# Hybrid conv / RWKV / MoE block on one core: weights laid out in load order, last norm's gain spread by TensorE, other pieces and rings at both ends

## The chip, the cores and the metric

The kernel runs on one core of one Trainium2 chip. The metric is the device time of one execution in microseconds (us), the median of several runs; work on the host before the launch is not in it. Names of engines are those of the profile: PE (matrix multiply), PEld (its weight loads), DVE, ACT, POOL, and SP, which here only issues DMA.

## The reference

One block over 256 tokens of width 2048, all in float32: a mixing half and a mixture of experts with 32 experts of inner width 512.

```
u = rms_norm(x, norm_mix);  proj = u @ w_in                  # w_in 2048 x 5408
y_conv = conformer_conv(proj[:1024], proj[1024:2048], ...)   # 31 taps
y_rwkv = rwkv7_time_mix(proj[2048:], ...)    # the last 288 columns of w_in are low-rank inputs
h = x + concat(y_conv, y_rwkv) @ w_out                       # w_out 2048 x 2048
v = rms_norm(h, norm_ffn)
h = h + moe(v)    # per token 2 of 32 experts:  (silu(v @ w_gate[e]) * (v @ w_up[e])) @ w_down[e]
out = rms_norm(h, norm_final)
```

Every expert has some token here, and the kernel loads all 32: w_gate and w_up (2048 x 512) and w_down (512 x 2048) are 4 MB each, so 403 MB in all.

## The kernel before

**Start.** `norm_in` loads x in four pieces of 512 KB and the 288 low-rank columns of w_in in four pieces, in the order of `STARTS`, squares and sums x, and multiplies the low-rank columns with x already (names `la`, `xn`), so that the statistics and these products lie side by side. The scale of each token is spread over the partitions by a matmul (`rstd`), and only then are the operands `yh` and `yl` of the big projections made.

**Mixing half.** `proj` computes 256 output columns at a time: chunks of 8 row blocks of a weight (128 x 2048 numbers, 1 MB) are loaded, split on ACT and DVE into a high and a low part (`hi`, `lo`), and multiplied three times. Its weights are w_in (20 column blocks, by two chunks each), then w_out (8 column blocks, in `w_out_pass`, the last two row blocks apart in `load_rest`).

**Experts.** They are taken in 16 pairs (`pair`). Both experts of a pair share PE: columns 0 to 63 are slots of one, 64 to 127 of the other. A pair has 24 chunks of 1 MB, in this order: four groups of gate, gate, up, up (one for each expert of the pair), then four quarters of w_down with two chunks each. PE multiplies group by group (tiles `g`, `u`), transposes the hidden layer (`hid`, `hT`), multiplies with w_down (`y`), and adds the rows back to their tokens with 0/1 matrices (`cb`, `acc`). The next pair's tokens are gathered (`gt`, `xe`) between these.

**Rings.** Chunks go to buffers in a fixed cycle of 21, written by `ORDER` from five groups: A, B, C, D and E. A is the ring that the first half streams its weights through (two of its buffers hold x until w_out is done), and `NA` and `NB` say how many A and B have. In the last pair A is taken out, for the last norm uses it (`final_tiles`), and the cycle goes on over what is left, by the chunk's number modulo the length:

```
def ORDER(A, B, C, D, E):
    return C[0:3] + B + A[0:2] + C[3:] + D + A[2:4] + E + A[4:]
r = rings[self.nchunk % len(rings)]                            # expert_chunk
rings = [r for r in rings if r[0] is not self.ring]            # last pair
```

All weights are issued by SP, in program order as the scheduler wrote it. A DMA there waits for the DMA that last used its completion counter (there are eight, taken in turn: the names DMAHW0 to DMAHW7 in the rows of the order below), for PE where the buffer's last reader is a matmul, and holds back everything behind it.

**End.** `expert_down` of the last pair works in the pieces of `LAST`, with `behind=0`: after each piece PE waits for ACT and DVE (`yh`, `yl`), then does its `cb`. `final_part` squares the sums on ACT and multiplies by the gain (`nfb`) on DVE; `final_norm` reduces, scales and stores. PE runs the experts in the order of the program.

Of the kernel before, what the change touches and what calls it, by code (L numbers as in the profile page):

```python
# [31 lines left out]
TAPS = -2500  # L32
LOW = -1500
GATHER = -24
STARTS = (0, 4, 1, 2, 3, 5, 6, 7)
PSTART = ("l0", "l1", "l2", "l3", "s0", "s1", "s2", "s3", "l4", "l5", "b", *(f"l{k}" for k in range(6, 16)))
TOKENS = ((0, 4), (4, 4), (8, 4), (12, 2), (14, 2))
WSLOT = {4: "ylb", 5: "yla", 6: 0, 7: 1}
RING = 1024
NA, NB, ND, NEX = 5, 7, 3, 1  # L40
NXE = 3
CHAIN = 400
QUARTERS = [(512 * i, 512) for i in range(4)]
LAST = QUARTERS[:2] + [(1024, 384), (1408, 384), (1792, 256)]
FINAL = [(i, slice(a, b)) for i in range(2) for a, b in ((0, 512), (512, 1024), (1024, 2048))]


def ORDER(A, B, C, D, E):
# [6 lines left out]
      "conv_b", "ln_g", "ln_b"]  # L55
PCI = {n: i for i, n in enumerate(PC)}
INPUTS = ["xT", "w_in", "w_out", "pc", "dw", "mul", "nmix", "nffn_c", "wa_up", "g_up1", "g_up2",
          "rw", "rb", "nffn_p", "nfin", "w_gate", "w_up", "w_down"]


def bcast_rows(ap, n):
    return bass.AP(tensor=ap.tensor, offset=ap.offset, ap=[[0, 128], [1, n]])
# [13 lines left out]
class Block:  # L76
# [169 lines left out]
        nc.vector.tensor_sub(lo, view, hi.bitcast(F32))  # L246
        return hi, lo

    def proj(self, src, k0, nk, c0, width, xh, xl, x0, cols, slot=None):
        accs = [self.bank(self.pacc, [128, 256], "acc") for _ in cols]  # L250
        rows = src.rearrange("(k p) n -> p k n", p=128)
        for b in range(0, nk, 8):
            nb = min(8, nk - b)
            with self.tc.high_priority(offset=2000):
                c = self.chunk(rows[:, k0 + b:k0 + b + nb, c0:c0 + width], slot)
            for g in range(0, nb, 4):
                ng = min(4, nb - g)
# [12 lines left out]
    def norm_in(self):  # L270
        nc = self.nc
        V, A = nc.vector, nc.scalar
        warm = self.tmp.tile([128, 1], F32, tag="t", name="warm")
        A.activation(warm, self.c_rms, AF.Sqrt)
        xr = self.xT.rearrange("(k p) t -> p k t", p=128)
        wr = self.w_in.rearrange("(k p) n -> p k n", p=128)
        x = lambda k, n: self.xT_s[k // 8][:, k % 8:k % 8 + n]
        wl = []
        for step in STARTS:
            if step < 4:  # L280
                nc.sync.dma_start(x(4 * step, 4), xr[:, 4 * step:4 * step + 4])
            else:
                k = 4 * (step - 4)
                c = self.chunk(wr[:, k:k + 4, O_L:O_L + 288])
                wl += [c[:, j] for j in range(4)]
        xn = [self.rwkv_parts(i, F32, "y") for i in range(2)]
        ss = self.bank(self.pmm, [128, 2], "mm")
        la = [self.bank(self.pacc, [128, 288], "acc") for _ in range(2)]
        sqs = []
        for g in range(4):  # L290
            for k in range(4 * g, 4 * g + 4):
                V.tensor_scalar(xn[k // 8][k % 8], self.xt(k), self.nmix_s[:, k:k + 1], None, op0=OP.mult)
            sq = self.spl.tile([128, 4, 256], F32, tag="hi" if g % 2 else "lo", name="nsq")
            A.activation(sq, x(4 * g, 4), AF.Square)
            V.tensor_add(sq[:, 0:2], sq[:, 0:2], sq[:, 2:4])
            V.tensor_add(sq[:, 0], sq[:, 0], sq[:, 1])
            sqs.append(sq)
        rs = self.lo.tile([128, 2], F32, name="rs")
        dg = self.tmp.tile([128, 2, 128], F32, tag="t", name="dg")
        rstd = self.bank(self.pmm, [128, 256], "mm")  # L300
        last = None

        def ordered(*a, **k):
            nonlocal last
            m = nc.tensor.matmul(*a, **k)
            if last is not None:
                self.after(m, last, sync=False)
            last = m

        for step in PSTART:  # L310
            n = int(step[1:] or 0)
            for i in range(2):
                ts = slice(128 * i, 128 * i + 128)
                if step[0] == "l":
                    ordered(la[i], xn[n // 8][n % 8][:, ts], wl[n], start=n == 0, stop=n == 15)
                elif step[0] == "s":
                    ordered(ss[:, i:i + 1], sqs[n][:, 0, ts], self.ones[:, 0:1],
                            start=n + i == 0, stop=n + i == 4)
                else:
                    if i == 0:  # L320
                        A.activation(rs, ss, AF.Sqrt, bias=self.c_rms, scale=1.0 / D)
                        self.gate_in = V.reciprocal(rs, rs)
                    V.tensor_scalar(dg[:, i], self.ident, rs[:, i:i + 1], None, op0=OP.mult)
                    ordered(rstd[:, ts], self.ones, dg[:, i], start=True, stop=True)
        yh, yl = (Parts([self.ypool.tile([128, 8, 256], F32R, tag=n + h, name=n + h) for h in "ab"], 8)
                  for n in ("yh", "yl"))
        for g in range(8):
            s = slice(2 * g, 2 * g + 2)
            y = xn[g // 4][2 * (g % 4):2 * (g % 4) + 2]
            V.tensor_mul(y, y, rstd[:, None, :].to_broadcast([128, 2, 256]))  # L330
            A.activation(yh[s], y, AF.Copy)
            self.gate_y = V.tensor_sub(yl[s], y, yh[s].bitcast(F32))
        self.yh, self.yl = yh, yl
        self.la, self.rs = la, rs
# [3 lines left out]
                      for h, n in (("a", 6), ("b", 2))], 6)  # L338

    def w_in_cols(self, c0):  # L340
        return self.proj(self.w_in, 0, 16, c0, 256, self.yh, self.yl, 0, (0, 128))

    def shift(self, ps, mu, omu, out):
        nc = self.nc
# [411 lines left out]

    def w_out_pass(self, k0, nk, xh, xl, x0, slots={}):
        for b in range(8):
            ps = self.proj(self.w_out, k0, nk, 256 * b, 256, xh, xl, x0, (0, 128), slots.get(b))
            for i in range(2):  # L760
                h = self.xt(2 * b + i)
                self.nc.vector.tensor_add(h, h, ps[i])

    def load_rest(self):
        self.wrest = []
        for k in (14, 15):
            c = self.ring.tile([128, 2048], F32, tag="w", name="w")
            self.nc.sync.dma_start(c, self.w_out[128 * k:128 * k + 128, :])
            self.wrest.append(c)

    def rest_block(self, b):
# [287 lines left out]
    def wsrc(self, which, e, q):  # L1059
# [1 line left out]
            w = (self.w_gate, self.w_up)[which][e]  # L1061
            return w.rearrange("(p a) f -> p a f", a=16)[:, 4 * q:4 * q + 4, :]
        c0, n = q
        return self.w_down[e].rearrange("(p a) n -> p a n", a=4)[:, :, c0:c0 + n]

    def expert_chunk(self, rings, which, e, q):
        r = rings[self.nchunk % len(rings)]
# [8 lines left out]

    def final_tiles(self):
        nfb, *self.fin = (self.ring.tile([128, D], F32, tag="w", name=n) for n in ("nfb", "fin0", "fin1"))
        self.nc.gpsimd.dma_start(nfb, bcast_rows(self.nfin, D))
        self.nfb = nfb  # L1080
        self.fs1 = self.per.tile([128, 2], F32, name="fs1")
        self.fss = self.per.tile([128, 2, len(LAST)], F32, name="fss")

    def final_part(self, c0, w):
        k = [c for c, _ in LAST].index(c0)
# [47 lines left out]
    def run(self):  # L1133
# [4 lines left out]
        with ExitStack() as top:  # L1138
# [6 lines left out]
            with P("yp", 1, "right") as self.ypool:  # L1145
# [25 lines left out]
                with ExitStack() as ex:  # L1171
# [19 lines left out]
                    with tc.manual_schedule(engines={mybir.EngineType.PE}):  # L1191
                        xe = [self.gather(wk, pg, S, 0, 2)]
                        late = ()
                        for pr in range(NE // 2):
                            load = lambda w, j, q: self.expert_chunk(rings, w, 2 * pr + j, q)
                            last = pr + 1 == NE // 2
                            if last:
                                rings = [r for r in rings if r[0] is not self.ring]
                                self.final_tiles()
                            xe, S, late = self.pair(wk, pg, py, pgu, load, (2 * pr, 2 * pr + 1), xe, S,  # L1200
                                                    None if last else (2 * pr + 2, 2 * pr + 3),
                                                    None if pr else weights, late,
                                                    **(dict(pieces=LAST, after=self.final_part, behind=0)
                                                       if last else {}))
                    self.final_norm()
            self.overflow()

# [1 line left out]
def pack(inputs):  # L1209
    g = {k: np.asarray(v) for k, v in inputs.items()}  # L1210
    f = {}
    f["xT"] = np.ascontiguousarray(g["x"][0].T)
    f["w_in"] = g["w_in"][0]
    f["w_out"] = g["w_out"][0]
    mu = g["shift_mu"][0]
    ch = {"mu_r": mu[0:DC], "mu_k": mu[DC:2 * DC], "mu_v": mu[2 * DC:3 * DC], "w0": g["w0"][0],
          "a0": g["a0"][0], "k_k": g["k_k"][0], "k_a": g["k_a"][0], "r_k": g["r_k"][0].reshape(-1),
# [18 lines left out]
    f["nfin"] = g["norm_final"][None]  # L1236
    f["w_gate"] = g["expert_w_gate"][0]
    f["w_up"] = g["expert_w_up"][0]
    f["w_down"] = g["expert_w_down"][0]
    return {n: f[n] for n in INPUTS}  # L1240


# [11 lines left out]
```

## Time and profile before

| what | value |
|---|---|
| time, median of 3 runs | 1495.16 us (1492.93 to 1495.94) |
| the profiled execution's own time | 1495.7 us |
| its span, first to last instruction | 1493.6 us |
| busy share of the span | PE 94%, PEld 58%, DVE 44%, ACT 27%, POOL 2% |
| chain that ended last | PE 56%, DMA 30%, DVE 10%, ACT 2% |
| HBM read | 468.97 MB, 315 GB/s over the span |
| granted clock of TensorE, mean | 0.99 |

The shares of busy time run over two unlike parts: until about 530 us the mixing half, in which the DMA engines are half idle, and from there on the experts, in which they are busy throughout. A PE that is busy is not a PE at its peak, since matmuls overlap. What limits a stretch is read from the chain and from windows over that stretch.

### The profile page before, as it was taken

Reading aid. Unit: us, or ns where it says so; the run is one execution under the profiler, and the core shown is the slowest. Engines: PE = TensorE matmul, PEld = TensorE weight load, DVE = VectorE, ACT = ScalarE, POOL = GpSimd, SP = SyncE. Lnnn points to the kernel's source line nnn. Section 1 sums busy time; section 2 is a strip of 40 time slices with the busy share of each in tenths; the row PEclk is TensorE's granted clock in tenths of the full one; section 3 lists DMA queues with packets and bytes.
Section 4 is the critical chain, followed back from the end, with each engine's and each line's share of the span. In section 5 each row is a group of like instructions: output and inputs, shape, how many; then the busy total and the mean of one; then the engine's idle time right before and its main releaser. Section 6 shows DMA issues by size and latency. Waiting matters only on the chain.

```text
span 1493.6 us, 21307 instructions
## 1 busy us (share of the span) xinstructions
PE 1402.4 (94%) x8730; PEld 859.6 (58%) x8730; DVE 656.4 (44%) x1350; ACT 409.9 (27%) x758; POOL 30.3 (2%) x66
## 2 busy tenths in 40 slices
PE   7999999999999979999999999999898998989895
PEld 5989988888889944434434434434344344433432
DVE  7797977969867533223223223222131231221314
ACT  5657666676685411001001001001000010000102
POOL 4000000000000000000000000000000000000000
PEclk9999999999999999999999999999999999999998
DMA  7542442432549779999999999999999999999993
GB/s 235 184 149 85 136 130 88 151 101 88 177 128 346 284 292 377 414 412 426 412 418 417 412 422 415 414 421 412 417 421 413 424 412 415 416 409 425 410 412 138
DMA packets 168518, 472.52 MB, mean 316 GB/s; under 512 B 8000, under 2 KB 70512, under 8 KB 135264
## 3 DMA queue, kind: packets, MB, share of 16 engines
q1 hardware_dynamic: 167072, 467.96, 80.4%
q0 software_dynamic: 1200, 3.13, 0.7%
q8 instruction: 71, 1.16, 0.3%
q14 instruction: 31, 0.25, 0.1%
q10 hardware_dynamic: 144, 0.01, 0.0%
HBM read 468.97 MB, written 2.10 MB: 315 GB/s over the span
## 4 chain that ended last, share of the span: by engine, by line
PE 56%; DMA 30%; DVE 10%; ACT 2%; issue 1%; SPq 0%; ACTq 0%; DVEq 0%
DMA w<-in_w_up_dram 21%; PE acc L217 14%; PE u L217 9%; PE y L217 9%; PE g L217 8%; DMA w<-in_w_down_dram 7%; PE mm L217 7%; PE gt L217 5%; PE cb L217 3%; DVE lo L246 3%; DVE mix L642 2%; DVE MB L479 1%; DMA w<-in_w_in_dram 1%; PE cn L217 1%; ACT hi L245 1%
## 5 line engine op out<-in xcount | busy, mean ns | idle before, releaser
L217 PE MATMUL u<-w,xe 128*64 128x512 f32 x1024 | 252.1, 600 | 22.4 <-DMA w<-in_w_up_dram 22.4
L217 PE MATMUL g<-w,xe 128*64 128x512 f32 x1024 | 248.0, 597 | 13.6 <-DMA w<-in_w_gate_dram 11.2
L217 PE MATMUL y<-w,hT 128*64 128x512 f32 (+2 forms) x1040 | 232.5, 594 | 0.7 <-ACT hT L1022 0.7
L1039 DVE TENSOR_TENSOR acc<-acc,cb 128x512 f32<-128x512 f32 (+2 forms) x130 | 86.0, 674 | 218.8 <-PE cb L217 218.8
L217 PEld LDWEIGHTS u<-w,xe 128*64 128x64 f32 x1024 | 81.7, 138 | 173.2 <-issue 129.2
L1014 DVE TENSOR_TENSOR hid<-sg,u 128x256 f32<-128x256 f32 x32 | 19.6, 614 | 346.6 <-PE u L217 346.6
L217 PEld LDWEIGHTS g<-w,xe 128*64 128x64 f32 x1024 | 73.9, 136 | 152.6 <-issue 121.8
L246 DVE TENSOR_TENSOR lo<-w,hi 128x1024 fp32r<-128x1024 f32 x108 | 127.6, 1181 | 46.5 <-ACT hi L245 33.8
L217 PEld LDWEIGHTS y<-w,hT 128*64 128x64 f32 x1040 | 70.6, 137 | 133.7 <-issue 118.3
L1010 ACT ACTIVATE sg<-g 128x512 f32<-128x512 f32 x16 | 9.6, 597 | 482.5 <-PE g L217 482.5
L217 PE MATMUL gt<-S,vt 128*128 128x128 f32 x1024 | 125.9, 279 | 6.8 <-DVE xe L961 5.2
L217 PEld LDWEIGHTS gt<-S,vt 128*128 128x128 f32 x1024 | 120.8, 194 | 14.3 <-DVE xe L961 8.7
L245 ACT ACTIVATE hi<-w 128x1024 fp32r<-128x1024 f32 x108 | 110.8, 1026 | 54.3 <-PE acc L217 45.5
L1052 ACT ACTIVATE yh<-y,gate 128x512 fp32r<-128x512 f32 (+2 forms) x65 | 44.3, 681 | 251.6 <-PE y L217 251.6
L642 DVE SCALAR_TENSOR_TENSOR mix<-UP,dw_s,mix 128x256 f32<-128x256 f32 x240 | 104.0, 477 | 2.7 <-ACT mix L640 2.4
L217 PE MATMUL acc<-yha,hi 128*128 128x256 f32 x320 | 92.1, 288 | 2.5 <-ACT hi L245 1.8
L217 PE MATMUL acc<-yla,hi 128*128 128x256 f32 x320 | 92.5, 289 | 0.0
L217 PE MATMUL acc<-yha,lo 128*128 128x256 f32 x320 | 92.0, 288 | 0.0
L217 PE MATMUL acc<-yhb,lo 128*128 128x256 f32 x320 | 91.9, 287 | 0.0
L217 PE MATMUL acc<-ylb,hi 128*128 128x256 f32 x320 | 91.2, 285 | 0.0
L217 PE MATMUL acc<-yhb,hi 128*128 128x256 f32 x320 | 90.3, 282 | 0.0
L961 DVE TENSOR_TENSOR xe<-gt,nffnp_s 128x512 f32<-128x512 f32 (+1 forms) x65 | 44.4, 683 | 80.9 <-PE gt L217 80.9
(352 smaller groups left out, 1894.2 us busy)
## 6 DMA issues: line engine op xcount, KB each, us to landing
w<-in_w_gate_dram SPq DMA_DIRECT2D x128, 1024.0 KB, 19.1
w<-in_w_up_dram SPq DMA_DIRECT2D x128, 1024.0 KB, 19.5
w<-in_w_down_dram SPq DMA_DIRECT2D x124, 1024.0 KB, 14.2
w<-in_w_in_dram SPq DMA_DIRECT2D x40, 1024.0 KB, 5.2
w<-in_w_out_dram SPq DMA_DIRECT2D x8, 1024.0 KB, 5.8
w<-in_w_out_dram SPq DMA_DIRECT2D x8, 768.0 KB, 4.7
w<-in_w_down_dram SPq DMA_DIRECT2D x4, 768.0 KB, 12.6
w<-in_w_in_dram SPq DMA_DIRECT2D x4, 576.0 KB, 7.4
```

The source lines that it names most:

```text
L217: self.nc.tensor.matmul(*a, **k)
L245: nc.scalar.activation(hi, view, AF.Copy)
L246: nc.vector.tensor_sub(lo, view, hi.bitcast(F32))
L479: V.copy_predicated(MB[:, 2 * h + c], self.mkP.rearrange("p a b -> p (a b)"), P12[h])
L642: V.scalar_tensor_tensor(c, u, d, c, op0=OP.mult, op1=OP.add)
L961: self.nc.vector.tensor_mul(xe[:, a:a + n], ps, self.nffnp_s[:, k0:k0 + n, None].to_broadcast([128, n, 128]))
L1010: A.activation(sg, gp, AF.Silu)
L1014: V.tensor_mul(hid, *(t.rearrange("s (p f) -> s f p", f=4)[:, f:f + 2] for t in (sg, up)))
L1039: V.tensor_add(a, a, cb)
L1052: A.activation(yh, yp, AF.Copy, scale=gate)
```

## The change

- The host stores x, w_in, w_out and w_down in the order in which the kernel loads them. Every load of them is then one unbroken run in HBM, with one long row for each partition (4 to 8 KB), where before a chunk had rows of 1 KB (w_in, w_out, x) or 2 KB (w_down). The numbers that land in SBUF are the same, except for the low-rank columns.
- The low-rank columns come in three loads of 6, 5 and 5 row blocks (before, four of 4), at other places among the pieces of x.
- Ring A has 6 buffers and ring B has 6 (before, 5 and 7). The cycle still has 21; without A the last pair's has 15 (before, 16).
- The gain of the last norm is loaded as one row, and four matmuls with a row of ones spread it over the partitions (`final_gain`, behind the first group of the last pair), with four ACT copies. Before, one DMA read the row 128 times.
- The last w_down goes in pieces of 512, 512, 512, 256 and 256 columns (before 512, 512, 384, 384, 256), and PE does a piece's `cb` after the next piece's `y`.

```
-STARTS = (0, 4, 1, 2, 3, 5, 6, 7)
+STARTS = (0, 4, 1, 2, 5, 3, 6)
+LORA = ((0, 6), (6, 5), (11, 5))
-NA, NB, ND, NEX = 5, 7, 3, 1
+NA, NB, ND, NEX = 6, 6, 3, 1
-LAST = QUARTERS[:2] + [(1024, 384), (1408, 384), (1792, 256)]
+LAST = QUARTERS[:3] + [(1536, 256), (1792, 256)]
...
-                c = self.chunk(rows[:, k0 + b:k0 + b + nb, c0:c0 + width], slot)
+                c = self.chunk(rows[:, k0 + b:k0 + b + nb], slot)
...
             if step < 4:
-                nc.sync.dma_start(x(4 * step, 4), xr[:, 4 * step:4 * step + 4])
+                nc.sync.dma_start(x(4 * step, 4), self.xT[step])
             else:
-                k = 4 * (step - 4)
-                c = self.chunk(wr[:, k:k + 4, O_L:O_L + 288])
-                wl += [c[:, j] for j in range(4)]
+                k, n = LORA[step - 4]
+                c = self.chunk(self.w_lo[:, k:k + n])
+                wl += [c[:, j] for j in range(n)]
...
-        return self.w_down[e].rearrange("(p a) n -> p a n", a=4)[:, :, c0:c0 + n]
+        return self.w_down[e, c0 // 512][:, :, c0 % 512:c0 % 512 + n]
...
-        self.nc.gpsimd.dma_start(nfb, bcast_rows(self.nfin, D))
+        self.nfr = self.fin[0][0:1, :]
+        self.nc.gpsimd.dma_start(self.nfr, self.nfin)
+        self.one_row = self.fin[1][0:1, 0:128]
+        self.nc.vector.memset(self.one_row, 1.0)
...
+    def final_gain(self, pg):
+        for c0, w in QUARTERS:
+            ps = self.bank(pg, [128, w], "gt")
+            self.mm(ps, self.one_row, self.nfr[:, c0:c0 + w], start=True, stop=True)
+            self.nc.scalar.activation(self.nfb[:, c0:c0 + w], ps, AF.Copy)
...
                                 self.final_tiles()
+                                late = [*late, lambda: self.final_gain(pg)]
...
-                                                    **(dict(pieces=LAST, after=self.final_part, behind=0)
-                                                       if last else {}))
+                                                    **(dict(pieces=LAST, after=self.final_part) if last else {}))
+                        for f in late:
+                            f()
...
+    f["w_in"] = np.ascontiguousarray(wi[:, 0:O_L].reshape(16, 128, 20, 256).transpose(2, 1, 0, 3))
+    f["w_lo"] = np.ascontiguousarray(wi[:, O_L:].reshape(16, 128, 288).transpose(1, 0, 2))
+    f["w_out"] = np.ascontiguousarray(wo[0:1792].reshape(14, 128, 8, 256).transpose(2, 1, 0, 3))
+    f["w_down"] = np.ascontiguousarray(
+        g["expert_w_down"][0].reshape(NE, 128, 4, 4, 512).transpose(0, 3, 1, 2, 4))
```

Three places show how the order of instructions moves. The first is SP at the start of the program. `xT_s` is x, `w` a buffer of ring A, and the last row in each is the 40 chunks of w_in. Before:

```order
L281 DMA xT_s<-in_xT_dram 128x4x256
L237 DMA w<-in_w_in_dram 128x4x288
L281 DMA xT_s<-in_xT_dram 128x4x256 x3
L237 DMA w<-in_w_in_dram 128x4x288 x3
L237 DMA w<-in_w_in_dram 128x8x256 x40
```

Now:

```order
L280 DMA xT_s<-in_xT_dram 128x1024
L238 DMA w<-in_w_lo_dram 128x1728
L280 DMA xT_s<-in_xT_dram 128x1024 x2
L238 DMA w<-in_w_lo_dram 128x1440
L280 DMA xT_s<-in_xT_dram 128x1024
L238 DMA w<-in_w_lo_dram 128x1440
L238 DMA w<-in_w_in_dram 128x2048 x40
```

The last piece of x now stands behind the second low-rank load, and one buffer is left over for the first chunk of w_in.

The second is SP where the last pair's loads begin, with what each DMA waits for in brackets (PE: a buffer's last reader). The rows of w_down are the last of the pair before. Before:

```order
L1074 DMA w<-in_w_down_dram 128x4x512 [waits DMAHW0_49,PE_49]
L1074 DMA w<-in_w_down_dram 128x4x512 [waits DMAHW1_49,PE_49]
L1074 DMA w<-in_w_down_dram 128x4x512 [waits DMAHW2_49,PE_49]
L1074 DMA w<-in_w_gate_dram 128x2048 [waits DMAHW3_49,PE_49]
L1074 DMA w<-in_w_gate_dram 128x2048 [waits DMAHW4_49,PE_49]
L1074 DMA w<-in_w_up_dram 128x2048 [waits DMAHW5_49,PE_49]
L1074 DMA w<-in_w_up_dram 128x2048 [waits DMAHW6_49,PE_49]
```

Now:

```order
L1073 DMA w<-in_w_down_dram 128x2048 [waits DMAHW7_49,PE_49]
L1073 DMA w<-in_w_down_dram 128x2048 [waits DMAHW0_49,PE_49]
L1073 DMA w<-in_w_down_dram 128x2048 [waits DMAHW1_49,PE_49]
L1073 DMA w<-in_w_gate_dram 128x2048 [waits DMAHW7_49,DMAHW2_49,PE_49]
L1073 DMA w<-in_w_up_dram 128x2048 [waits DMAHW3_49]
L1073 DMA w<-in_w_gate_dram 128x2048 [waits DMAHW4_49,DMAHW0_49,PE_49]
L1073 DMA w<-in_w_up_dram 128x2048 [waits DMAHW5_49,DMAHW1_49,PE_49]
L1073 DMA w<-in_w_gate_dram 128x2048 [waits DMAHW6_49]
```

The last pair's first, third and fourth load now wait for counters 7, 0 and 1 as well, which are those of the three w_down loads just ahead; and one up chunk stands ahead of the second gate chunk.

The third is PE after the last pair's transposes of `hid`. Before, the end of the program was:

```order
L217 MATMUL y<-w,hT 64x512 x8
L217 MATMUL cb<-yh,ST 128x512
L217 MATMUL cb<-yl,ST 128x512
L217 MATMUL cb<-yh,ST 128x512
L217 MATMUL cb<-yl,ST 128x512
L217 MATMUL y<-w,hT 64x512 x8
```

Now:

```order
L218 MATMUL y<-w,hT 64x512 x16
L218 MATMUL cb<-yh,ST 128x512
L218 MATMUL cb<-yl,ST 128x512
L218 MATMUL cb<-yh,ST 128x512
L218 MATMUL cb<-yl,ST 128x512
L218 MATMUL y<-w,hT 64x512 x8
```

Two pieces of `y` now stand ahead of the first `cb`, and so on to the end, where two groups of `cb` follow each other.

## Rows read from the trace of the kernel before

**Rows 1.** The page: what the DMA engines moved, span in 40 slices.

```profile
GB/s 235 184 149 85 136 130 88 151 101 88 177 128 346 284 292 377 414 412 426 412 418 417 412 422 415 414 421 412 417 421 413 424 412 415 416 409 425 410 412 138
```

**Rows 2.** Windows over the experts; at the right PEclk, DMA share, GB/s.

```profile
530.00:550.00 20.00, 18.07 (x92) 9.49 (x94) 5.87 (x28) 1.59 (x3) 0.00 (x0) 0.88 0.56 207
590.00:900.00 310.00, 308.27 (x1558) 133.74 (x1556) 77.87 (x153) 21.70 (x33) 0.00 (x0) 1.00 1.02 416
```

**Rows 3.** The chain in order of time, experts: start us, us, what.

```profile
634.25 7.02 PE y L217 x32
...
854.41 7.02 PE y L217 x32
...
917.94 19.58 DMA w<-in_w_up_dram
...
957.27 3.65 PE u L217 x14
...
1017.70 3.65 PE u L217 x14
```

**Rows 4.** Windows: w_down moving (963 to 975), gate and up (the others).

```profile
924.00:951.00 27.00, 27.00 (x131) 11.67 (x128) 4.81 (x10) 0.69 (x1) 0.00 (x0) 1.00 1.01 426
963.00:975.00 12.00, 11.65 (x71) 6.45 (x70) 3.71 (x8) 1.49 (x3) 0.00 (x0) 1.00 1.05 394
981.00:1011.00 30.00, 28.73 (x138) 11.20 (x134) 5.90 (x12) 0.69 (x1) 0.00 (x0) 1.00 1.01 425
```

**Rows 5.** The start: the chain in order of time, and one window.

```profile
1.31 5.73 DMA w<-in_w_in_dram
20.07 8.43 DMA w<-in_w_in_dram
32.01 0.55 PE mm L362 x3
5.40:12.00 6.60, 4.83 (x10) 3.50 (x11) 5.80 (x17) 4.05 (x5) 1.48 (x6) 1.00 1.09 351
```

**Rows 6.** The start: the timeline of DVE and ACT.

```profile
18.14 1.88 DVE L330 TENSOR_TENSOR y0a<-y0a,mm 128x512 f32<-128x512 f32 x3 [0.17 <-PE mm L305]
31.48 0.87 ACT L360 ACTIVATE mix<-acc,rs 128x288 f32<-128x288 f32 x2
```

**Rows 7.** The gain's tile `nfb`, and the chain while it loads.

```profile
L1079 POOL DMA_DIRECT2D nfb<-in_nfin_dram x1: 533/533/533, 1376.5 to 1376.5; - x1
...
1363.41 22.16 DMA w<-in_w_up_dram
```

**Rows 8.** PE's timeline over the ends of two pairs; idle before it in brackets.

```profile
1322.14 3.65 PE L217 MATMUL u<-w,xe 128*64 128x512 f32 x14 [1.34 <-DMA w<-in_w_up_dram]
1340.64 3.65 PE L217 MATMUL y<-w,hT 128*64 128x512 f32 x16
1345.35 3.65 PE L217 MATMUL y<-w,hT 128*64 128x512 f32 x16
1385.62 6.55 PE L217 MATMUL u<-w,xe 128*64 128x512 f32 x14 [3.74 <-DMA w<-in_w_up_dram]
```

**Rows 9.** SP's timeline, last pair; DMA issues from 514.2 to 515.2, us to landing.

```profile
1410.72 5.04 SPq L1074 DMA_DIRECT2D w<-in_w_gate_dram  x2
...
w<-in_w_up_dram SPq DMA_DIRECT2D x1, 1024.0 KB, 5.0
```

**Rows 10.** The end: PE's timeline, and two rows of the chain.

```profile
1452.70 5.35 PE L217 MATMUL y<-w,hT 128*64 128x512 f32 x16 [0.74 <-ACT hT L1022]
1460.53 3.65 PE L217 MATMUL y<-w,hT 128*64 128x512 f32 x16
1476.49 1.95 PE L217 MATMUL y<-w,hT 128*64 128x256 f32 x16
861.43 1.12 PE cb L217 x4
1481.83 0.08 DVE fs L1095
```

More of the change, by code (lines that the diff above doesn't have):

```diff
@@ L57 @@
 INPUTS = ["xT", "w_in", "w_out", "pc", "dw", "mul", "nmix", "nffn_c", "wa_up", "g_up1", "g_up2",
-          "rw", "rb", "nffn_p", "nfin", "w_gate", "w_up", "w_down"]
+          "rw", "rb", "nffn_p", "nfin", "w_lo", "w_outr", "w_gate", "w_up", "w_down"]
 def bcast_rows(ap, n):
@@ L247, in split, with proj @@
         return hi, lo
-    def proj(self, src, k0, nk, c0, width, xh, xl, x0, cols, slot=None):
+    def proj(self, rows, k0, nk, xh, xl, x0, slot=None):
+        cols = (0, 128)
         accs = [self.bank(self.pacc, [128, 256], "acc") for _ in cols]
-        rows = src.rearrange("(k p) n -> p k n", p=128)
         for b in range(0, nk, 8):
@@ L274, in norm_in @@
         A.activation(warm, self.c_rms, AF.Sqrt)
-        xr = self.xT.rearrange("(k p) t -> p k t", p=128)
-        wr = self.w_in.rearrange("(k p) n -> p k n", p=128)
         x = lambda k, n: self.xT_s[k // 8][:, k % 8:k % 8 + n]
@@ L340, in w_in_cols @@
     def w_in_cols(self, c0):
-        return self.proj(self.w_in, 0, 16, c0, 256, self.yh, self.yl, 0, (0, 128))
+        return self.proj(self.w_in[c0 // 256], 0, 16, self.yh, self.yl, 0)
     def shift(self, ps, mu, omu, out):
@@ L758, in w_out_pass @@
         for b in range(8):
-            ps = self.proj(self.w_out, k0, nk, 256 * b, 256, xh, xl, x0, (0, 128), slots.get(b))
+            ps = self.proj(self.w_out[b], k0, nk, xh, xl, x0, slots.get(b))
             for i in range(2):
@@ L765, in load_rest @@
         self.wrest = []
-        for k in (14, 15):
+        for k in range(2):
             c = self.ring.tile([128, 2048], F32, tag="w", name="w")
-            self.nc.sync.dma_start(c, self.w_out[128 * k:128 * k + 128, :])
+            self.nc.sync.dma_start(c, self.w_outr[128 * k:128 * k + 128])
             self.wrest.append(c)
@@ L1211, in pack @@
     f = {}
-    f["xT"] = np.ascontiguousarray(g["x"][0].T)
-    f["w_in"] = g["w_in"][0]
-    f["w_out"] = g["w_out"][0]
+    f["xT"] = np.ascontiguousarray(g["x"][0].T.reshape(4, 4, 128, T).transpose(0, 2, 1, 3))
+    wi, wo = g["w_in"][0], g["w_out"][0]
+    f["w_in"] = np.ascontiguousarray(wi[:, 0:O_L].reshape(16, 128, 20, 256).transpose(2, 1, 0, 3))
+    f["w_lo"] = np.ascontiguousarray(wi[:, O_L:].reshape(16, 128, 288).transpose(1, 0, 2))
+    f["w_out"] = np.ascontiguousarray(wo[0:1792].reshape(14, 128, 8, 256).transpose(2, 1, 0, 3))
+    f["w_outr"] = np.ascontiguousarray(wo[1792:])
     mu = g["shift_mu"][0]
@@ L1238, in pack @@
     f["w_up"] = g["expert_w_up"][0]
-    f["w_down"] = g["expert_w_down"][0]
+    f["w_down"] = np.ascontiguousarray(
+        g["expert_w_down"][0].reshape(NE, 128, 4, 4, 512).transpose(0, 3, 1, 2, 4))
     return {n: f[n] for n in INPUTS}
```

## The prediction, made before the result

> **What bounds the kernel now.** I read the page's slices first. In [rows 1] the slices of 37 us show a DMA rate of 85 to 346 GB/s in the first fourteen, the mixing half, and of 409 to 426 from the sixteenth to the one before the last. The first windows [rows 2] confirm it: at 530 us, where the experts begin, the DMA engines are at 0.56 of their time (the 21 buffers are full), and from 590 to 900 at 1.02. So the experts are a stream of loads at full rate. The chain says otherwise at first sight: up to 900 us it runs through PE, and a pair takes (854.41 - 634.25) / 4 = 55.04 us; only from 918 us does it run through DMA, with 1017.70 - 957.27 = 60.43 us a pair [rows 3]. Both hold. PE lives on the backlog of full buffers and eats it up, while the loads are never faster than DMA allows. The last load's landing is therefore fixed by the DMA stream from about 560 us on, and what shortens a load counts in every pair after that, in those too whose chain names PE.
>
> The time is then made of four parts: when the stream starts, what it takes, what holes are in it, and what PE does after the last landing.
>
> **The stream: w_down in 8 KB rows.** In the windows of [rows 4] gate and up move at 425 to 426 GB/s, that is 1.0486 MB / 425.5 = 2.464 us a chunk. The window with w_down in it shows 394 GB/s at a DMA share no lower (1.05): the engines are not idle, they move less. By the pair's 60.43 us the eight w_down chunks take 60.43 - 16 x 2.464 = 21.0, or 2.625 us each. After the change their rows are as long as those of gate and up, so I give them 2.464 as well: 0.16 us each. It counts for pairs 1 to 14, 112 chunks: pair 0's are loaded while buffers are full, and the last pair's land behind the last up chunk, beside PE's work. 112 x 0.16 = 17.9; I take 17, for a little goes where the ring is full. The bounds are 0 (rows of 2 KB cost nothing and the 394 has another cause) and 24: eight up and w_down chunks in the chain's 19.58 us [rows 3] are 2.45 each, and 394 GB/s makes 2.66 at the other end, 0.21 x 112. A pair then takes 16 x 2.464 + 8 x 2.464 = 59.1, still above PE's 55.04.
>
> The Trainium skill, "DMA: Bandwidth & Descriptors", section Specifications, says that a transfer reaches line rate from 512 bytes on. By it rows of 2 KB have nothing to gain, and the sum would end at 1491. This trace does not agree: rows of 1 KB ran at 351 GB/s [rows 5], 2 KB at 394, 8 KB at 425. It is a rival below.
>
> **The start.** In the chain [rows 5] the first w_in chunk is issued at 20.07, because its buffer (ring A's) was a low-rank load's and PE had to read it first, and lands at 28.50; PE, which stood idle before, goes on from 32.01. Now a sixth buffer of A is free for it, so it follows the other start loads at once. x and the low-rank columns are 4.46 MB, the chunk 1.05. A lone load takes 5.0 us [rows 9], of which 2.46 are the transfer, so about 2.5 are latency; from 1.31 + 2.5 on, 5.5 MB at 425 GB/s (long rows) take 13.0: it lands at about 17. The scale of the tokens comes a little later, since the last piece of x stands behind the second low-rank load: 3.72 MB at 425 land at 12.6, against 2.69 MB at 351 (11.5) before, so I put the scaling 0.9 us after the 18.14 of [rows 6]: 19.0. From there DVE is the chain. Those three operations took 1.88, 0.63 each; some 12 like them and one split of a 1 MB half (twice the size, 1.25) stand ahead of what PE's low-rank transposes need: 19.0 + 8.8 = 27.8. One more split of the operand on ACT (0.6) and the start of ACT's copies `mix` (0.5) make 28.9; PE began 0.53 after `mix` in before (31.48 to 32.01), so now at 29.4. Gain 2.6. The bounds are 0 (DVE and ACT fill the gap) and 8.4 (the whole wait for the chunk). Everything after it on all engines stands in the same order up to w_out's end, so the experts start that much earlier, and the stream with them. The longer rows of w_in and w_out are worth nothing by themselves: the DMA engines have room there [rows 1].
>
> **The gain.** `nfb` is issued at 1376.5 and 1 MB of writes goes beside the stream; in the chain the load that it meets takes 22.16 us in place of 19.58 [rows 7]. Gone: 2.5. Its replacement is one 8 KB row and four matmuls of 512 columns in float32. No matmul of plain float32 with 512 columns stands in the trace. A run of 16 of the kernel's own, in its faster format, takes 3.65 [rows 8]; four at that pace are 0.9, and I take four times as much, 3.6, an estimate (at the slower pace of the 14 at 1385.62 it would be up to 7.5). In a DMA-bound pair PE waits 3.7 us anyway [rows 8], which is the cover: they cost nothing unless that slack is used up, as the next part says.
>
> **The hole before the last pair.** Chunk 360 is the last pair's first. With 15 buffers in its ring 360 mod 15 = 0: chunks 360 to 362 go to C0, C1 and C2. The pairs before use 21 buffers, and 336 mod 21 = 0, so chunks 357 to 359, the three w_down loads just ahead, lie in those same buffers. The order shows it as the double waits on DMAHW7, 0 and 1. Before, 360 mod 16 = 8 pointed to a B buffer, long free, and the same two waits fell on the pair's ninth and tenth load: SP stood there too, 5.04 us [rows 9], but loads were in flight behind it. Now SP stops at the first load, until PE has done the third quarter of `y`. In [rows 8] the last up chunk's landing starts `u` at 1322.14, and that quarter ends at 1340.64 + 3.65 = 1344.3, or 22.1 later (the last one at 26.9). What is already issued are the eight w_down chunks, and they are drained 8 x 2.45 = 19.6 after that landing. The engines then wait 22.1 - 19.6 = 2.5 and another 2.3 of latency: a hole of 4.8 us. Behind SP wait all loads of the last pair, and PE for them: its third load lands about 32 after that landing, 4 us after PE is out of work. The clock falls on such idling: after 3.74 us of it 14 matmuls took 6.55 in place of 3.65 [rows 8], 2.9 more. Part of it, and of the gain's 3.6, comes back because loads run on meanwhile. I take 5.5 for all (bounds 0, if SP's wait is over before the eight loads are; 8, if clock and gain come on top of half the hole).
>
> **The tail.** From the first `y` of the last w_down at 1452.70 to the end of the last one at 1476.49 + 1.95 = 1478.44 PE took 25.7 [rows 10], with a wait for `yh` and `yl` ahead of every `cb`. With `cb` one piece behind, PE has work throughout: 5.35 + 3.65 + 1.12 + 3.65 + 1.12 + 1.95 + 1.12 + 1.95 = 19.9, or 19.7 with shorter last `cb`: 6.1 earlier. After it come the last `yl`, two `cb`, and DVE's queue of sums and gains, which is now closer packed: the 3.4 from the last `y` to `fs` at 1481.83 grows, I think by 1.7, as one more piece's sums stand ahead of it. Gain 4.4 (bounds 2, if DVE is the bound, and 6.1).
>
> **Sum.** -17 - 2.6 - 2.5 + 5.5 - 4.4 = -21.0. The profiled execution took 1495.7 (span 1493.6 and 2.1 around it), which is 0.5 above the median of the runs shown; so 1495.2 - 21.0 = 1474.
>
> **The rivals.**
> 1. *No hole.* PE's `y` quarters end while the eight w_down loads still run, SP's wait hides itself. For it: 2.5 us is a small difference of two long sums. Against it: the loads also get shorter, which drains them sooner. 1474 - 5.5 = 1468.5.
> 2. *A deep hole.* The idle PE falls to the lower clock, and the gain's matmuls and the first groups run at it, so that PE becomes the bound of the last pair: 2.9 more for one group and up to 7.5 - 3.6 for the gain's matmuls, of which the 5.5 holds some already: 1478 to 1481.
> 3. *Rows of 2 KB are no slower.* The 394 GB/s would come from SP's or PE's rhythm. Against it: a DMA share of 1.05 in that window. The stream's 17 fall away: 1491, still 0.3% faster. The rule of the Trainium skill named above leads here.
> 4. *Slower.* The unbroken 1 MB of w_down reads worse than the interleaved one: the engines might then ask HBM for neighbouring pieces at once. Place: the 112 chunks. The other terms give 4.0; w_down must then cost 7 us more in all, 0.06 a chunk (2.69 us, 390 GB/s), for the kernel to be 0.2% slower. At the worst rate that the trace shows, 351 GB/s [rows 5], or 2.99 us, it is 112 x 0.365 = 41 more: 1532. Against it: gate and up are unbroken chunks already and run at 425.
>
> **How the numbers follow.** Forecast 0.66, no hole 0.13, deep hole 0.11, no gain from rows 0.07, slower 0.03. The likeliest case's own range is 1468 to 1480, from the bounds of w_down (24 against 17), start and tail. With the first two rivals the range is 1465 to 1484; what lies outside is the last two and the far ends, about 2 in 10 at most. A change of under 0.2% (3 us) can't be told from none in this kernel. Faster by more: 0.66 + 0.13 + 0.11 and most of 0.07, 0.94; same 0.03; slower 0.03.
>
> **What the changed profile would show.** Stream: windows with w_down at about 425 GB/s, and a pair's period near 59.1. Start: PE's transposes of `mix` at about 29.4, and the first w_in chunk issued well before 20. Gain: no load of 22 us in the chain near 1360. Hole: SP waiting at the first gate chunk of the last pair, no DMA traffic for about 5 us, and PE idle ahead of `g`, with a low granted clock behind. Tail: `y` and `cb` without idle time between, and about 20 us from the first `y` to the end of the last. Wrong it is if w_down stays at 394, or if the stream turns out to be held by PE before the last pair, so that shorter loads only fill buffers sooner.

## The result and the profile after

| | before | after |
|---|---|---|
| time, median | 1495.09 us (1492.93 to 1495.94, 4 runs) | 1475.68 us (1472.64 to 1478.68, 4 runs) |
| ratio to before | | 0.9872, 95% interval 0.9849 to 0.9896 |
| profiled execution, own time | 1495.7 us | 1478.68 us |
| its span | 1493.6 us | 1477.0 us |

The change makes the kernel 19.4 us faster by the medians; 21 was forecast. The profiled execution is the slowest of the four, 3.0 us above the median, so the parts below add up to the 17 us between the two profiled executions.

The page's row of the DMA rate, the span in 40 slices:

```profile
GB/s 276 176 151 89 146 120 89 152 94 90 179 137 349 237 274 381 425 423 425 425 424 424 425 424 424 425 425 425 423 426 424 424 425 425 423 424 425 336 428 152
```

In [rows 1] the experts' slices move between 409 and 426 GB/s; now they stand at 423 to 428, but for the last, as before, and for one, the third from the end, with 336. That one is the hole. Windows of the same stretches as [rows 2] and [rows 4] (at the right PEclk, DMA share, GB/s):

```profile
590.00:900.00 310.00, 308.27 (x1558) 133.42 (x1554) 77.10 (x152) 21.03 (x32) 0.00 (x0) 1.00 1.01 424
924.00:951.00 27.00, 27.00 (x133) 10.62 (x133) 4.81 (x10) 0.21 (x1) 0.00 (x0) 1.00 1.01 426
963.00:975.00 12.00, 12.00 (x56) 4.34 (x54) 3.23 (x5) 2.07 (x3) 0.00 (x0) 1.00 1.01 426
981.00:1011.00 30.00, 30.00 (x145) 11.94 (x142) 2.98 (x8) 0.60 (x1) 0.00 (x0) 1.00 1.01 425
```

No window is slower than another any more. The chain in order of time (start us, us, what), two pairs in the middle and the last pair's start:

```profile
1107.45 19.76 DMA w<-in_w_up_dram
1127.28 19.57 DMA w<-in_w_down_dram
1146.92 19.63 DMA w<-in_w_up_dram
1166.61 19.64 DMA w<-in_w_up_dram
...
1388.57 3.61 PE y L218 x16
1392.17 6.14 DMA w<-in_w_gate_dram
```

A pair takes 1166.61 - 1107.45 = 59.16 us where it took 60.43 [rows 3]; 59.1 was forecast. No load of 22 us stands in the chain, as one did in [rows 7]. At the last pair the chain goes through `y`, and then through a load whose issue waited for it. The two longest of SP's waits from 1360 to 1395 (line, what it waited for, us, times, the longest), and three windows of that place:

```profile
SPq L1073 <- DMA w<-in_w_down_dram: 14.5, 1, 14.5
SPq L1073 <- PE y L218: 10.8, 2, 7.3
...
1384.00:1388.00 4.00, 4.00 (x19) 1.41 (x16) 1.35 (x3) 0.53 (x1) 0.00 (x0) 1.00 0.04 14
1396.00:1400.00 4.00, 1.64 (x4) 0.53 (x6) 0.00 (x0) 0.00 (x0) 0.00 (x0) 0.56 1.01 422
1400.00:1404.00 4.00, 4.00 (x14) 1.22 (x12) 0.00 (x0) 0.00 (x0) 0.00 (x0) 0.58 1.01 426
```

At the last pair's first load SP stands for 14.5 us on the counter of a w_down load, while the loads already issued run on, and then for 7.3 us on PE. From 1384 to 1388 the DMA engines move 14 GB/s. PE pays later: from 1396 to 1400 it is busy for 1.64 of 4 us, and its granted clock is 0.56, near the lower of its two levels. PE's timeline over the place (idle time before in brackets):

```profile
1365.27 3.65 PE L218 MATMUL u<-w,xe 128*64 128x512 f32 x14 [1.21 <-DMA w<-in_w_up_dram]
...
1388.49 3.65 PE L218 MATMUL y<-w,hT 128*64 128x512 f32 x16
...
1393.22 1.07 PE L218 MATMUL g<-w,xe 128*64 128x512 f32 x2
1398.36 5.67 PE L218 MATMUL g<-w,xe 128*64 128x512 f32 x13 [4.06 <-DMA w<-in_w_gate_dram]
...
1408.95 3.79 PE L218 MATMUL gt<-fin,fin 1*128 1x512 f32 x8
1412.67 2.98 PE L218 MATMUL gt<-S,vt 128*128 128x128 f32 x16
1415.58 4.33 PE L218 MATMUL g<-w,xe 128*64 128x512 f32 x16
...
1440.20 8.78 PE L218 MATMUL y<-w,hT 128*64 128x512 f32 x32 [0.73 <-ACT hT L1021]
...
1457.79 1.95 PE L218 MATMUL y<-w,hT 128*64 128x256 f32 x16
```

After those 4.06 us PE waits for nothing until the transposes ahead of 1440.20: it does not catch up with the loads again. From the last `u` of the pair before to the first `y` of the last pair it is 1440.20 - 1365.27 = 74.9 us; before it was 1452.70 - 1385.62 = 67.1 [rows 8, 10]. That is 7.8 more, although the eight w_down loads in between are shorter now. The tail is shorter: the chain's `fs`, next, stands 24.9 behind the first `y`, against 1481.83 - 1452.70 = 29.1 [rows 10].

```profile
1465.07 0.08 DVE fs L1103
```

### The profile page after: what moved, and what is told of

It is laid out like the page before. It is cut to its first block, busy times and chain, and to the rows that moved or that the text cites. A ratio compares the mean times of both kernels' runs of the same rounds, so it can differ in the third digit from the quotient of the medians.

```text
span 1477.0 us, 21321 instructions
## 1 busy us (share of the span) xinstructions
PE 1401.5 (95%) x8738; PEld 855.7 (58%) x8738; DVE 656.1 (44%) x1351; ACT 413.0 (28%) x762; POOL 35.7 (2%) x66
## 4 chain that ended last, share of the span: by engine, by line
PE 57%; DMA 26%; DVE 12%; ACT 2%; issue 1%; SPq 0%; ACTq 0%; DVEq 0%
DMA w<-in_w_up_dram 17%; PE acc L218 12%; PE y L218 10%; PE g L218 9%; PE u L218 9%; DMA w<-in_w_down_dram 8%; PE mm L218 7%; PE gt L218 5%; DVE lo L247 3%; PE cb L218 3%; DVE mix L641 2%; DVE MB L478 1%; ACT hi L246 1%; PE cn L218 1%; DVE xe L960 1%
## 5 line engine op out<-in xcount | busy, mean ns | idle before, releaser
L218 PE MATMUL u<-w,xe 128*64 128x512 f32 x1024 | 244.9, 593 | 10.8 <-DMA w<-in_w_up_dram 10.5
L218 PE MATMUL y<-w,hT 128*64 128x512 f32 (+1 forms) x1040 | 232.2, 594 | 0.7 <-ACT hT L1021 0.7
L1038 DVE TENSOR_TENSOR acc<-acc,cb 128x512 f32<-128x512 f32 (+1 forms) x130 | 86.4, 675 | 227.3 <-PE cb L218 227.3
L218 PEld LDWEIGHTS u<-w,xe 128*64 128x64 f32 x1024 | 76.6, 137 | 162.4 <-issue 137.2
L1013 DVE TENSOR_TENSOR hid<-sg,u 128x256 f32<-128x256 f32 x32 | 19.6, 614 | 325.3 <-PE u L218 325.3
L1051 ACT ACTIVATE yh<-y,gate 128x512 fp32r<-128x512 f32 (+1 forms) x65 | 44.3, 682 | 251.4 <-PE y L218 251.4
## 6 DMA issues: line engine op xcount, KB each, us to landing
w<-in_w_gate_dram SPq DMA_DIRECT2D x128, 1024.0 KB, 19.6
w<-in_w_up_dram SPq DMA_DIRECT2D x128, 1024.0 KB, 19.6
w<-in_w_down_dram SPq DMA_DIRECT2D x126, 1024.0 KB, 19.6
```

The source lines that it names most:

```text
L218: self.nc.tensor.matmul(*a, **k)
L1013: V.tensor_mul(hid, *(t.rearrange("s (p f) -> s f p", f=4)[:, f:f + 2] for t in (sg, up)))
L1038: V.tensor_add(a, a, cb)
L1051: A.activation(yh, yp, AF.Copy, scale=gate)
```

## The experiments

All twelve compare with the kernel before, run beside them on the same chip; times are medians.

**The last pair's ring begun elsewhere.**

```
-rings = [r for r in rings if r[0] is not self.ring]
+rings = [r for r in rings[3:] + rings[:3] if r[0] is not self.ring]
```

> The changed kernel with the last pair's cycle of 15 begun at ring B in place of ring C, so that its first three loads go to buffers that were used 21 chunks ago. Hole theory: SP does not wait at the last pair's first load, the DMA engines run on at about 425 GB/s, the last up chunk lands 4.7 us earlier, PE does not idle 4 us ahead of the first group and keeps the clock, and the four matmuls of the gain lie in PE's slack: 5 to 8 us faster than the changed kernel, 1468 to 1471. Rival (PE bounds the last pair whatever the loads do): less than 2 us, 1474 to 1476.

1469.7 us, ratio 0.9832 (0.9816 to 0.9848): 6.0 faster than the changed kernel, the fastest of all. PE's timeline:

```profile
1365.67 3.65 PE L218 MATMUL u<-w,xe 128*64 128x512 f32 x14 [1.44 <-DMA w<-in_w_up_dram]
...
1393.59 3.65 PE L218 MATMUL g<-w,xe 128*64 128x512 f32 x16
...
1401.73 3.79 PE L218 MATMUL gt<-fin,fin 1*128 1x512 f32 x8
...
1408.05 4.65 PE L218 MATMUL g<-w,xe 128*64 128x512 f32 x16
...
1432.99 7.09 PE L218 MATMUL y<-w,hT 128*64 128x512 f32 x32 [0.74 <-ACT hT L1021]
```

And the window in which the changed kernel moved 14 GB/s:

```profile
1384.00:1388.00 4.00, 4.00 (x19) 1.30 (x18) 1.76 (x3) 0.12 (x1) 0.00 (x0) 1.00 1.01 426
```

PE goes from the last `y` into `g` without a wait, and from `u` to `y` it is 1432.99 - 1365.67 = 67.3 us, 7.6 less than in the changed kernel. The hole theory holds, in place and in size. Two parts of the expectation did not come. The clock falls behind the gain's matmuls (last section), and those matmuls do not lie in PE's slack: without them the distance is 65.9 (the run with the broadcast, below). That 67.3 is close to the 67.1 of the kernel before is chance, since the w_down loads were longer there.

**The hole put into the kernel before.**

```
 rings = [r for r in rings if r[0] is not self.ring]
+rings = rings[8:] + rings[:8]
```

> The kernel before with its last pair's cycle of 16 turned by half, so that its first loads go to C0, C1 and C2, used by the three w_down loads just ahead. Hole theory: w_down takes 2.62 us a chunk here, so eight of them drain 21.0 us after the last up chunk and the hole is 22.1 - 21.0 + 2.3 = 3.4 us, and up to 3 us more where PE falls to the lower clock: 1498.5 to 1501.5. Rival (the place in the ring costs nothing, since other loads are in flight): 1495.

1502.43 us, ratio 1.0046 (1.0032 to 1.006): 7.7 us slower than the kernel before beside it, 1 us more than expected at most. The hole's rows:

```profile
1387.59 5.34 PE L217 MATMUL u<-w,xe 128*64 128x512 f32 x14 [3.57 <-DMA w<-in_w_up_dram]
...
1421.63 4.92 PE L217 MATMUL g<-w,xe 128*64 128x512 f32 x13 [3.34 <-DMA w<-in_w_gate_dram]
...
1461.67 3.65 PE L217 MATMUL y<-w,hT 128*64 128x512 f32 x16 [0.74 <-ACT hT L1022]
```

From 1408 to 1412 the DMA engines move 5 GB/s. The distance is 74.1 us, 7.0 more than in [rows 8, 10]. The size was missed because the `u` at 1387.59, slowed as in [rows 8], took 5.34 us in place of 3.65: the third quarter of `y` ends 23.8 us after the start of `u`, not 22.1, and SP waits for it.

**`cb` at once.**

```
-dict(pieces=LAST, after=self.final_part)
+dict(pieces=LAST, after=self.final_part, behind=0)
```

> The changed kernel with each cb of the last w_down straight behind its own piece of y again (the pieces stay 512, 512, 512, 256 and 256). Tail theory: five waits of 0.85 to 1.1 us ahead of cb come back on PE, less 1.7 us that DVE's queue gives back: 3 to 4.5 us slower than the changed kernel, 1478.5 to 1480. Rival (DVE's sums and gains bound the tail): 1 us at most.

1482.55 us, ratio 0.9918 (0.9904 to 0.9932): 6.9 above the changed kernel by the medians, more than expected, but the intervals leave room for 4, and the two profiled executions are 3.9 apart. Its profile: the first `y` at 1439.96, and

```profile
1446.65 0.50 PE L218 MATMUL cb<-yl,ST 128*128 128x512 f32 x1 [0.29 <-DVE yl L1052]
...
1468.83 0.09 DVE fs L1103
```

28.9 us from `y` to `fs` against 24.9: 4.0. The waits on `yh` and `yl` are back (0.79 and 0.29 here), and DVE is not the bound.

**Rings of 5 and 7.**

```
-NA, NB, ND, NEX = 6, 6, 3, 1
+NA, NB, ND, NEX = 5, 7, 3, 1
```

> The changed kernel with 5 buffers in ring A and 7 in B. The first w_in chunk has to wait for a low-rank load's buffer again, and the last pair's cycle is 16 long, so its first load goes to a B buffer. Theory: the experts start 2 to 3 us later than in the changed kernel, and the hole with what hangs on it (5 to 8) is gone: 1470 to 1473. Rival on the start (the gain came from the long rows, not from the buffer): experts start within 0.5 us of the changed kernel's 528.5.

1471.77 us, ratio 0.9852 (0.9837 to 0.9868): the hole is gone, as expected. The start is not as expected. The first w_in chunk waits for its buffer (SP issues it at 18.51; in the changed kernel at 4.51), and still the experts start at 527.23, where the changed kernel has 528.47. The two starts differ in the granted clock too, which from 14 to 24 us is 1.00 here and 0.83 there. Three other runs with the changed kernel's start have 1.00 as well, and their experts start at 526.6 to 527.4: the buffer is worth less than 1 us. My theory of the start falls with this run.

**The rows of w_down: length or place.** Four layouts in HBM for pairs 0 to 14, in the changed kernel otherwise as it is. The old one is rows of 2 KB, 8 KB apart; the others keep a chunk in one unbroken 1 MB and cut its rows (in short; the names differ from run to run):

```
+w_dr = w_down.reshape(NE, 128, 4, 4, nb, m).transpose(0, 3, 2, 4, 1, 5)   # m = 512, 256, 128 numbers
-return self.w_down[e, c0 // 512][:, :, c0 % 512:c0 % 512 + n]
+return self.w_dr[e, c0 // 512].rearrange("a p b -> p a b")
```

> The changed kernel with w_down of pairs 0 to 14 laid out as before: rows of 2 KB, 8 KB apart, so that a 1 MB chunk is spread over 4 MB. Row theory (the stream's term): w_down falls back to 394 to 404 GB/s, a pair takes 60.4 us again, the last up chunk lands 15 to 17 us later, less 1 us or so of a smaller hole: 1488 to 1492. Rival (rows of 512 bytes and more run at one rate): 1476, with windows at 425 GB/s.

> As the run with the old rows, but the rows of 2 KB of a chunk lie close together in one unbroken 1 MB (four blocks of 128 rows). Row theory (a row costs, wherever it lies): as the old layout, 394 to 404 GB/s and 1488 to 1492. Rival (it was the spread over 4 MB): 425 GB/s and 1476.

> w_down of pairs 0 to 14 in rows of 1 KB within an unbroken 1 MB. Row theory with one price for each row: 384 more rows cost 0.14 to 0.16 us a chunk, so 896 more cost 0.33 to 0.37: 2.8 us a chunk, 370 to 375 GB/s, and 37 to 42 us on 112 chunks: 1512 to 1518. Rival (one rate from 512 bytes on): 1476.

> w_down of pairs 0 to 14 in rows of 512 bytes within an unbroken 1 MB. Row theory with one price for each row: 1920 more rows, 0.70 to 0.80 us a chunk, 320 to 330 GB/s, 78 to 90 us on 112 chunks: 1554 to 1566. Rival (one rate from 512 bytes on): 1476.

1492.97 us (ratio 0.9995, 0.9985 to 1.0005), 1492.88 (0.9985, 0.9974 to 0.9995), 1514.65 (1.0137, 1.0111 to 1.0164) and 1561.38 (1.045, 1.0421 to 1.0479). The row theory holds in all four, with the first two 1 us above its range, and the rival's 1476 is far off. One window of each, in this order:

```profile
590.00:900.00 310.00, 308.27 (x1565) 134.55 (x1562) 77.57 (x154) 21.02 (x32) 0.00 (x0) 1.00 1.03 416
```

```profile
590.00:900.00 310.00, 308.26 (x1559) 133.55 (x1558) 77.46 (x153) 21.02 (x32) 0.00 (x0) 1.00 1.03 416
```

```profile
590.00:900.00 310.00, 305.09 (x1535) 132.31 (x1532) 75.91 (x150) 20.43 (x31) 0.00 (x0) 1.00 1.04 404
```

```profile
590.00:900.00 310.00, 300.34 (x1482) 131.47 (x1480) 76.64 (x152) 20.41 (x31) 0.00 (x0) 0.99 1.02 383
```

A pair moves 24 x 1.0486 = 25.17 MB. At 424, 416, 404 and 383 GB/s that is 59.4, 60.5, 62.3 and 65.7 us; the eight w_down chunks carry the difference, 0.14, 0.37 and 0.79 us each. Divided by the rows that they have more than the changed kernel's 128 (384, 896 and 1920), it is 0.37, 0.41 and 0.41 ns a row. Between the two places tried for rows of 2 KB there is no difference; the number of rows costs in proportion, and the DMA engines stay busy all the time. (By the kernel's layouts not every load of the change is one unbroken run: the 8 KB rows of a w_in chunk lie 16 KB apart, and those of gate and up, which the prediction took for unbroken chunks, 32 KB apart. Gate and up run at 425 to 426 GB/s, as the unbroken w_down does now.) The row of the Trainium skill, "DMA: Bandwidth & Descriptors", section Specifications, by which 512 bytes are enough for line rate, does not hold for these loads: 512 bytes in a third of the traffic cost 86 us.

**The start: rows or loads.** Two runs. In the first, x, the low-rank columns and w_in have their old layouts; in the second only the number and order of the low-rank loads and the rings are old:

```
-c = self.chunk(self.w_lo[:, k:k + n])
+c = self.chunk(self.w_in.rearrange("(k p) n -> p k n", p=128)[:, k:k + n, O_L:O_L + 288])
...
```

```
-STARTS = (0, 4, 1, 2, 5, 3, 6)
-LORA = ((0, 6), (6, 5), (11, 5))
-NA, NB = 6, 6
+STARTS = (0, 4, 1, 2, 3, 5, 6, 7)
+LORA = ((0, 4), (4, 4), (8, 4), (12, 4))
+NA, NB = 5, 7
```

> The changed kernel with x, the low-rank columns and w_in in the old layouts (rows of 1 KB and 1152 bytes); the three low-rank loads, their places and the rings stay as changed. The run with rings of 5 and 7 has shown that the free buffer did not make the gain at the start. Theory A (the long rows of the start's loads did): experts start 2 to 3 us later than in the changed kernel's 528.5, at 530.5 to 531.5, and the time is 1477.5 to 1479. Theory B (the number and places of the low-rank loads did): experts start within 0.7 us of 528.5, and the time is 1475 to 1477.

> The changed kernel with the low-rank columns in four loads at their old places and rings of 5 and 7, so that the start is that of before but for its long rows. The last pair's first load goes to a B buffer, so there is no hole. Theory A (long rows): experts start at 527 to 529, time 1470 to 1473 as with rings of 5 and 7 alone. Theory B (number and places of the low-rank loads): experts start at 530.5 to 531.5, time 1473.5 to 1476.

1479.34 us (0.9897, 0.9882 to 0.9912) with experts from 530.79, and 1474.7 (0.9867, 0.9852 to 0.9882) with experts from 530.05. The first comes out near theory A, the second near theory B. Each undoing takes most of the gain away, so neither is right alone; each was profiled once. In the four-load start the first w_in chunk is slow although its rows are long; in the three-load start with short rows it is the clock that is low, at 0.50 from 18 to 22 us:

```profile
18.79 8.72 DMA w<-in_w_in_dram
```

```profile
18.00:22.00 4.00, 4.00 (x10) 2.85 (x11) 1.89 (x9) 1.28 (x2) 3.25 (x6) 0.50 0.27 67
```

**The gain by broadcast again**, on the kernel with the turned ring:

```
-self.nc.gpsimd.dma_start(self.nfr, self.nfin)
+self.nc.gpsimd.dma_start(nfb, bcast_rows(self.nfin, D))
...
-late = [*late, lambda: self.final_gain(pg)]
```

> The kernel with the turned cycle (no hole), with the last norm's gain read 128 times by one DMA again and no matmuls for it. Gain theory: the load of the stream that the broadcast meets takes about 22 us, the last up chunk lands 2.5 us later than with the turned cycle alone; PE is rid of 3.8 us of matmuls that held it 1.5 us behind the loads there, so the sum is 0.5 to 1.5 us slower: 1470 to 1471.5. Rival (the matmuls of the gain and the clock behind them bound the last pair): 1 us or more faster, below 1468.7.

1470.59 us, ratio 0.9843 (0.983 to 0.9856), as expected. The chain has the long load again, and in the last pair PE has nothing slowed until the last `y`:

```profile
1343.40 22.14 DMA w<-in_w_up_dram
...
1365.58 3.65 PE L218 MATMUL u<-w,xe 128*64 128x512 f32 x14 [0.62 <-DMA w<-in_w_up_dram]
...
1431.43 8.62 PE L218 MATMUL y<-w,hT 128*64 128x512 f32 x32 [0.74 <-ACT hT L1021]
...
1404.00:1408.00 4.00, 4.00 (x22) 1.37 (x20) 0.25 (x1) 0.00 (x0) 0.00 (x0) 1.00 1.01 426
1408.00:1412.00 4.00, 4.00 (x20) 1.29 (x18) 0.00 (x0) 0.00 (x0) 0.00 (x0) 1.00 1.01 428
```

From `u` to `y` it is 65.9 us, the distance of a last pair that the loads bound; with the gain's matmuls it was 67.3.

**x ahead of the second low-rank load**, on the kernel with the turned ring:

```
-STARTS = (0, 4, 1, 2, 5, 3, 6)
+STARTS = (0, 4, 1, 2, 3, 5, 6)
```

> The kernel with the turned cycle (no hole), and all four pieces of x loaded ahead of the second low-rank load. Clock theory on the start: in half of the profiles PE waits some 2 us for the squares of x's last piece and falls to the lower clock from 17 to 22 us, which puts PE's first w_in products at 30.5 to 31.2 in place of 28.9. With x's last piece earlier there is no such wait; the clock stays at 1.00, the transposes of mix come at 28.9 or before and experts start at 526 to 527.5: 1467 to 1469. Rival (PE then waits for the second low-rank load instead, or DVE holds the start): experts start at 528 to 530 as with the turned cycle alone, 1469 to 1471.

1471.33 us, ratio 0.9843 (0.9829 to 0.9856): no gain over the turned ring alone. The clock from 14 to 24 us is 1.00 and the experts start at 526.68, as the clock theory has it (only the transposes of `mix`, expected by 28.9, come at 32.70, behind a POOL step, `rw_s`, in the chain). The gain at the start, 2.3 us against the turned ring's profile, is more than given back in the last pair:

```profile
1400.14 5.03 PE L218 MATMUL gt<-fin,fin 1*128 1x512 f32 x8
1405.09 3.78 PE L218 MATMUL gt<-S,vt 128*128 128x128 f32 x16
...
1433.01 8.78 PE L218 MATMUL y<-w,hT 128*64 128x512 f32 x32 [0.74 <-ACT hT L1021]
```

PE, not the loads, bounds this last pair, and it runs on the lower clock behind the gain's matmuls and again in `y`.

## Why the prediction was right, and where it was not

The time, 1475.68, lies 1.7 us above the forecast of 1474 and within the likeliest case's own range. That it is so near is partly luck: the profiled execution lies 4.7 above the forecast, mostly by the hole, and the other three were 2.0 to 6.0 us faster than it, which no profile explains. By the two profiled executions:

| term | forecast | measured | from |
|---|---|---|---|
| stream, 112 w_down chunks | -17 | -16.1 | last `u` of pair 14, 1385.62 to 1365.27, is -20.35; less the two rows below, it is -14.9 for the 104 chunks loaded by then (pairs 1 to 13), 0.144 each |
| start | -2.6 | -2.9 | first gather of the experts, 531.38 before, 528.47 after |
| gain's broadcast | -2.5 | -2.5 | 22.16 in the chain [rows 7], 19.6 now |
| hole | +5.5 | +9.0 | 67.1 to 74.9, and 1.2 for pair 14's eight chunks, which are shorter now |
| tail | -4.4 | -4.3 | 29.1 to 24.9 |
| sum | -21.0 | -16.8 | own times: 1495.7 to 1478.68, -17.0 |

- *Stream.* Right, a little oversized: 0.144 us a chunk, not 0.152 (17 / 112). The four layouts show the mechanism and give 0.14. The oversizing came from one pair's 60.43 us set against the best windows' rate; over 310 us the rates are 416 [rows 2] and 424, which is 60.5 and 59.4 us a pair.
- *Hole.* Right in place, cause and first size: 4.8 us without loads and 4 of idle PE were forecast, and PE's row has 4.06. But the term as a whole, 9.0, lies above its upper bound of 8. What was undersized is what follows. Part of the clock's and the gain's time, I wrote, "comes back because loads run on meanwhile". It did not: PE stayed behind the loads to the end of the pair, so its idle time, its slow matmuls and the gain's 3.79 all counted. Against the 65.9 us of a pair bound by the loads, the gain's matmuls cost 1.4 (67.3, the turned ring) and the hole 7.6 more (74.9). This is the mechanism of the rival "a deep hole", at a time that belongs to the likeliest case. The turned ring gives 6.0 back by the medians and 8.8 by the two profiled executions, in which `y` took 8.78 and 7.09.
- *Start.* The size was right and the step that led to it wrong. I held the free buffer of ring A for the cause; with rings of 5 and 7 the chunk waits for a buffer and the experts start less than 1 us later at the same clock. The transposes of `mix` came at 30.64, not at 29.4, which is 1.4 earlier than before; the other 1.5 lie between them and the experts, where the forecast had nothing, and no run separates them. What the runs show is that neither the long rows nor the three loads give the gain alone. The size also varies. Eight profiles have the changed kernel's start: in five of them, the changed kernel's among them, the clock is 0.83 from 14 to 24 us and the experts start at 528.5 to 529.7; in three it is 1.00 and they start at 526.6 to 527.4. So against 531.38 (532.06 in the run with the hole put into the kernel before, whose start is the same) the gain is 1.7 to 2.9 us with the lower clock and 3.9 to 4.8 without it. Why the first chunk takes 8.72 us in the four-load start and about 5.5 with rings of 5 and 7 is not settled; POOL's small loads are in flight beside it in both.
- *Gain.* The 2.5 us are confirmed twice. The price of the four matmuls was forecast at 3.6 and is 3.79 (the profile has eight instructions for the four). That they cost nothing in the DMA-bound pair was too kind: even without the hole, PE ends the pair behind the loads, 1.4 us later than without them, and with the broadcast instead the time is the same within the intervals.
- *Tail.* Right in size and mechanism: 19.5 us from the first `y` to the end of the last, and 5.3 from there to `fs`, where 19.7 and 5.1 were forecast. The run with `cb` at once gives 4.0 back in its profile.
- *The rivals.* No gain from rows, and slower, are excluded by the windows at 424 to 426 GB/s. "No hole" did not happen. "A deep hole" did, as said above.

## What to carry to other kernels

When a cycle of buffers gets another length, work out which buffer the first load after the switch meets, and who read it last: a wait at the first of a run of loads empties the DMA queue (14 GB/s in the changed kernel), while the same wait at the ninth, in the kernel before, left the DMA engines at 418 GB/s or more (from 1404 to 1416). In a stream of loads that is bound by the DMA engines, count the rows: here each row of a 1 MB load cost about 0.4 ns, and the two places tried for them made no difference. And a hole in the loads is not only as long as its idle time: what PE loses by the lower clock behind it comes on top, if PE has no slack left before the end.

## What was not expected of the hardware

The granted clock fell without any idle time of PE. With the turned ring PE works without a wait into the last pair's tail, and the windows behind the gain's matmuls, which read a single partition, are

```profile
1404.00:1408.00 4.00, 4.00 (x20) 2.68 (x18) 0.00 (x0) 1.54 (x3) 0.00 (x0) 0.84 1.01 426
1408.00:1412.00 4.00, 4.00 (x15) 1.33 (x16) 0.69 (x1) 0.00 (x0) 0.00 (x0) 0.74 1.01 428
```

where the same stretch with the broadcast has 1.00 in both. The `g` behind them took 4.65 us in place of 3.65. With x loaded first the window from 1404 to 1408 stands at 0.50, the lower level, with PE busy for all of its 4 us, and with rings of 5 and 7 at 0.55. No run separates the single partition from the plain float32 of these matmuls. At the start, an idle time of 2.00 us ahead of the squares was followed by the lower clock, and one of 1.69 us in the broadcast run was not:

```profile
16.03 0.58 PE L304 MATMUL mm<-ones,nsq 128*128 128x1 f32 x4 [2.00 <-DVE nsq L295]
16.47 3.17 PE L304 MATMUL acc<-w,y0a 128*128 128x288 f32 x8
```

```profile
15.96 0.58 PE L304 MATMUL mm<-ones,nsq 128*128 128x1 f32 x4 [1.69 <-DVE nsq L295]
16.40 2.19 PE L304 MATMUL acc<-w,y0a 128*128 128x288 f32 x8
```

The length of this wait alone does not tell the profiles apart: 0.93 us in the run with `cb` at once and 1.31 in the one with short rows at the start were followed by the lower clock too (0.69 and 0.76 from 15 to 18 us).
